# The first feed-forward product of a transformer block: left forms side by side, 512 columns to a matmul, and two of four weight sums by accumulating DMAs

## The chip, the cores and the metric

The kernel runs on one core of one Trainium2 chip. The metric is the device time of one execution in microseconds. The engines are named as the profile names them: PE (TensorE matmuls), PEld (its weight loads), DVE (VectorE), ACT (ScalarE), POOL (GpSimd) and SP (SyncE, which issues most DMAs).

## What is computed

One residual block over 512 tokens with 2048 features, in float32: two kinds of attention, then a feed-forward part, then a norm. The change concerns the feed-forward part:

```python
h2 = rmsnorm(x, g_mlp[l])
u = jax.nn.relu(jnp.einsum('bsd,df->bsf', h2, w_up[l]))     # 512 x 2048 times 2048 x 8192
x = x + jnp.einsum('bsf,fd->bsd', u * u, w_down[l])         # 512 x 8192 times 8192 x 2048
return rmsnorm(x, g_final)
```

## The kernel before

**Numbers.** Every float32 factor is split into a high half (the value rounded to the type that PE multiplies, made by a copy on ACT, L60) and a low half (the rest, made by a subtraction on DVE, L61, which waits for the copy). A product is then three matmuls that add into the same PSUM tile: high x high, low x high and high x low (`mm3`, L92 to L95). The program's scheduler sets the order in which each engine's instructions stand, and each engine runs its own in that order.

**First feed-forward product.** It uses seven products in place of eight (Strassen's scheme in Winograd's form). The left factor is the transposed activation, cut in four blocks and combined to seven forms by `a_form` (L449 on), one for each product `p`. Each form has a tile of high halves `fh{p}` and one of low halves `fl{p}`, both [128, 8, 256]: 8 chunks of the sum, 256 columns (tokens). They are made at the end of the output projection and stay for the whole product.

The right factor is `w_up`, taken in 32 units (`Unit`) of 256 columns each. A unit loads two raw tiles `wu` of 1 MB: b11 and b12 side by side in one, b21 and b22 in the other (five such buffers, pool `rw`; the first tile of unit 0 is two tiles `wq`). `Unit.product(p)` does one of the seven products: it makes the weight sum in place on DVE if the form needs one (p = 5, 6, 4, 7 at L557, L559, L561, L563), splits the sum into `wh` and `wl` (or `wx`, a fourth pair of buffers), multiplies (8 chunks x 3 matmuls of 256 columns into the accumulators `psa`, `psb` or `psc`), and combines the results. Products 1, 6, 7 and 4 add up in `psa`, which ACT copies out after 1, 6 and 7 (L572) and 4 (L582); DVE adds the copies to `psb` or `psc` (L578, L580, L584). The four results are rectified and squared on ACT (L585, L586).

The loop over units does product 1 of the new unit, 4 of the old one, 5 and 6 of the new, 3 of the old, 2 and 7 of the new. Between them `store_form` makes the forms for the second feed-forward product from each pair of units and stores them to DRAM (`ufd<-st`), so DVE, ACT and SP's DMA queue have that work as well.

**Around it.** Ahead of it stands the output projection (PSUM tiles `acco`), in four column blocks; at the end of each the residual tile `x2` is transposed, scaled to `hr`, turned into forms, and squared on ACT into a tile `junk` for the norm's sums (L509). Behind it comes the second feed-forward product (`accd`), with 512 columns to a matmul.

Of the kernel before, what the change touches and what calls it, by code (L numbers as in the profile page):

```python
# [35 lines left out]
def block_kernel(ctx, tc, x, g_attn, w_in, b_f, g_out_sb, g_out_fox, w_out, g_mlp, w_up, w_down, g_final, y):  # L36
# [407 lines left out]
    F = {p: tuple(form.tile([P, KC // 2, 2 * P], F32R, tag=f"f{c}{p}", name=f"f{c}{p}") for c in "hl") for p in range(1, 8)}  # L444
# [7 lines left out]
    def a_form(p, c, out, s=None):  # L452
# [4 lines left out]
        if p == 5:  # L457
            dve.tensor_tensor(s, a21, a22, op=ALU.add)
# [4 lines left out]
        if p == 3:  # L463
            dve.tensor_tensor(a12, a12, s, op=ALU.subtract)
# [4 lines left out]
    for n in range(4):  # L469
# [33 lines left out]
        for p in (1, 5, 6, 2, 7, 4, 3):  # L503
            if n == 3 and p == 4:
                break
            a_form(p, hr, [f[:, 2 * n:2 * n + 2, :] for f in F[p]], s12)
        for t in range(TB):
            junk = xp.tile([P, NT], F32, tag="junk", name="junk")
            act.activation(junk, x2[:, t, :], AF.Square, accum_out=ss2[:, t, n:n + 1])  # L509
# [7 lines left out]
    rw = ctx.enter_context(tc.tile_pool(name="rw", bufs=5, side="right", reuse_waits="tile"))  # L517
    ups_cm = tc.tile_pool(name="ups", bufs=2, space=PSUM, reuse_waits="tile")
# [11 lines left out]

    class Unit:
        def __init__(self, u):
            self.u = u
            cols = slice(2 * u * P, 2 * (u + 1) * P)
            rows_ = w_up.rearrange("(a i p) f -> i p a f", i=2, p=P)
            if u == 0:
# [10 lines left out]
            self.A, self.B, self.C = (ups.tile([P, NT], F32, tag=c, name=f"ps{c}")[:, :2 * P] for c in "abc")  # L547

        def product(self, p):
# [6 lines left out]
            if p == 5:  # L556
                dve.tensor_tensor(b11, b12, b11, op=ALU.subtract)  # L557
            if p == 6:
                dve.tensor_tensor(b11, b22, b11, op=ALU.subtract)  # L559
            if p == 4:  # L560
                dve.tensor_tensor(b21, b21, b11, op=ALU.subtract)  # L561
            if p == 7:
                dve.tensor_tensor(b12, b22, b12, op=ALU.subtract)  # L563
# [3 lines left out]
            for a in range(KC // 2):  # L567
                mm3(ps, hi[:, a, :], lo[:, a, :], F[p][0][:, a, :], F[p][1][:, a, :], a == 0 and p in (1, 2, 5), a == KC // 2 - 1)
            t1, t2 = slice(0, 2 * P), slice(2 * P, NT)
            if p in (1, 6, 7):  # L570
                self.m = sm.tile([P, 2 * P], F32, tag="m6" if p == 6 else "m", name=f"s{p}", bufs=2 if p == 6 else 1)
# [3 lines left out]
                if p == 1:  # L575
                    self.m1 = self.m
            if p == 7:
                dve.tensor_tensor(self.c[:, 1, t2], self.m, self.C, op=ALU.add)  # L578
# [289 lines left out]
```

## Time and profile before

| | |
|---|---|
| runs of the kernel | 2093.0, 2093.42, 2095.84 us; median 2093.42 |
| profiled execution | span 2090.6 us from the first to the last instruction; the median run is 2.8 us above it |
| output projection with its forms | about 640 to 829 us |
| first feed-forward product | about 829 to 1465 us |
| second feed-forward product | about 1465 to 2024 us |
| granted PE clock | 1.00 in these stages |

A group's row in the profile gives the line, the engine, the operation, out<-in with sizes, the count, the busy time, the mean duration of one, and then the engine's idle time just before with what ended it. Matmuls are pipelined, so the duration of one is longer than the interval from one to the next. In the kernel's sums a stream's interval is therefore taken: a stretch divided by the matmuls in it.

### The profile page before, as it was taken

To read this page: it belongs to the slowest core of one execution; us is meant where nothing else is said; L and a number is where in the kernel's file an instruction comes from. 1 tells how busy PE (TensorE), PEld (TensorE's weight loads), DVE (VectorE), ACT (ScalarE), POOL (GpSimd) and SP (SyncE) were. 2 spreads that over 40 slices of the span, in tenths; PEclk is the share of its full clock that TensorE was granted. 3 is DMA by queue.
4 is the path that set the end of the run, shared out by engine and by line. 5 is a ranking of instruction groups with operands and counts; after the bars stand their busy time and mean duration, and the time that the engine had idled before them with its cause. 6 is when DMAs were issued, how large, how long until landed. Compare 5 with 4: busy or idle time off the path is not lost.

```text
span 2090.6 us, 29838 instructions
## 1 busy us (share of the span) xinstructions
PE 2070.1 (99%) x12084; PEld 1841.0 (88%) x12084; DVE 1570.7 (75%) x1744; ACT 1034.2 (49%) x1396; POOL 52.9 (3%) x76
## 2 busy tenths in 40 slices
PE   9999999999999999999999999999999999999998
PEld 8888888888898888999999999999888888888886
DVE  5454545665677567888888888888798988888886
ACT  6333334444445555556665666666744443333433
POOL 0000000010000000000000000000000000000003
PEclk9999999999999999999999999999999999999999
DMA  6323332323323444466566566567856664663732
GB/s 193 81 87 85 83 89 72 90 75 87 81 81 111 147 145 152 138 206 192 185 219 189 185 205 205 176 201 248 299 201 251 249 225 172 249 250 134 271 111 81
DMA packets 239930, 339.68 MB, mean 162 GB/s; under 512 B 7936, under 2 KB 154416, under 8 KB 233776
## 3 DMA queue, kind: packets, MB, share of 16 engines
q1 hardware_dynamic: 238832, 335.64, 48.9%
q8 instruction: 95, 1.56, 0.3%
q10 hardware_dynamic: 960, 2.13, 0.3%
q14 instruction: 43, 0.35, 0.0%
HBM read 272.20 MB, written 65.54 MB: 162 GB/s over the span
## 4 chain that ended last, share of the span: by engine, by line
PE 98%; DVE 1%; ACT 0%; issue 0%; DMA 0%; SPq 0%; ACTq 0%
PE accd L93 8%; PE accd L94 8%; PE accd L95 8%; PE psa L94 6%; PE psa L93 6%; PE psa L95 6%; PE accq L95 6%; PE accq L94 6%; PE accq L93 6%; PE psc L94 3%; PE psc L95 3%; PE psc L93 3%; PE acco L95 3%; PE acco L94 3%; PE acco L93 3%; PE accv L93 3%
## 5 line engine op out<-in xcount | busy, mean ns | idle before, releaser
L60 ACT CAST wh<-wu 128x1024 fp32r<-128x1024 f32 x164 | 170.9, 1048 | 134.8 <-PE psa L94 55.3
L61 DVE TENSOR_TENSOR wl<-wu,wh 128x1024 fp32r<-128x1024 f32 x164 | 199.4, 1221 | 45.0 <-ACT wh L60 44.7
L94 PE MATMUL psa<-fl,wh 128*128 128x256 f32 x776 | 219.8, 283 | 1.8 <-DVE fl L61 1.8
L93 PE MATMUL psa<-fh,wh 128*128 128x256 f32 x776 | 219.9, 283 | 0.5 <-ACT s L572 0.5
L95 PE MATMUL psa<-fh,wl 128*128 128x256 f32 x776 | 219.7, 283 | 0.0
L61 DVE TENSOR_TENSOR wl<-wraw,wh 128x1024 fp32r<-128x1024 f32 (+2 forms) x133 | 158.7, 1194 | 80.1 <-ACT wh L60 73.8
L60 ACT CAST wh<-wd 128x1024 fp32r<-128x1024 f32 (+1 forms) x136 | 134.6, 999 | 168.6 <-PE accd L95 107.5
L60 ACT CAST wh<-wraw 128x1024 fp32r<-128x1024 f32 (+2 forms) x133 | 135.4, 1019 | 156.5 <-PE accq L94 77.6
L95 PE MATMUL accq<-hH,wl 128*128 128x512 f32 x512 | 200.4, 391 | 0.0
L93 PE MATMUL accq<-hH,wh 128*128 128x512 f32 x512 | 200.1, 391 | 0.0
L94 PE MATMUL accq<-hL,wh 128*128 128x512 f32 x512 | 200.0, 391 | 0.0
L61 DVE TENSOR_TENSOR wl<-wd,wh 128x1024 fp32r<-128x1024 f32 (+1 forms) x136 | 155.5, 1153 | 41.9 <-ACT wh L60 41.4
L93 PE MATMUL accd<-wh,uf 128*128 128x512 f32 x436 | 169.7, 389 | 0.9 <-issue 0.9
L94 PE MATMUL accd<-wl,uf 128*128 128x512 f32 x436 | 169.6, 389 | 0.0
L95 PE MATMUL accd<-wh,uf 128*128 128x512 f32 x436 | 169.6, 389 | 0.0
L94 PEld LDWEIGHTS psa<-fl,wh 128*128 128x128 f32 x776 | 149.0, 192 | 2.2 <-DVE fl L61 2.2
L60 ACT CAST wx<-wd 128x1024 fp32r<-128x1024 f32 (+1 forms) x88 | 87.5, 1000 | 127.3 <-PE accd L95 75.9
L93 PEld LDWEIGHTS psa<-fh,wh 128*128 128x128 f32 x776 | 149.0, 192 | 1.0 <-ACT s L572 0.7
L95 PEld LDWEIGHTS psa<-fh,wl 128*128 128x128 f32 x776 | 149.0, 192 | 0.2 <-DVE wl L61 0.2
L61 DVE TENSOR_TENSOR wx<-wd,wx 128x1024 fp32r<-128x1024 f32 (+1 forms) x88 | 100.7, 1153 | 23.6 <-ACT wx L60 23.2
L94 PEld LDWEIGHTS accq<-hL,wh 128*128 128x128 f32 x512 | 96.2, 188 | 19.5
L95 PEld LDWEIGHTS accq<-hH,wl 128*128 128x128 f32 x512 | 96.1, 188 | 19.3
(300 smaller groups left out, 5491.9 us busy)
## 6 DMA issues: line engine op xcount, KB each, us to landing
wu<-in_w_up_dram SPq DMA_DIRECT2D x63, 1024.0 KB, 6.7
ufd<-st SPq DMA_DIRECT2D x98, 512.0 KB, 6.8
wd<-in_w_down_dram SPq DMA_DIRECT2D x48, 1024.0 KB, 6.1
wraw<-in_w_in_dram SPq DMA_DIRECT2D x84, 512.0 KB, 3.7
uf<-ufd SPq DMA_DIRECT2D x42, 1024.0 KB, 5.9
wraw<-in_w_out_dram SPq DMA_DIRECT2D x32, 512.0 KB, 3.6
wd<-in_w_down_dram SPq DMA_DIRECT2D x16, 768.0 KB, 6.2
uf<-ufd SPq DMA_DIRECT2D x14, 768.0 KB, 5.6
```

What stands on the lines that cost most here:

```text
L60: ins = act.copy(hi, src)
L61: lows[0] = dve.tensor_tensor(lo, src, hi.bitcast(F32), op=ALU.subtract)
L93: pe.matmul(out, sh, mh, start=first, stop=False, skip_group_check=True)
L94: pe.matmul(out, sh, ml, start=False, stop=False, skip_group_check=True)
L95: pe.matmul(out, sl, mh, start=False, stop=last, skip_group_check=True)
```

## The change

```diff
-    F = {p: tuple(form.tile([P, KC // 2, 2 * P], F32R, tag=f"f{c}{p}", name=f"f{c}{p}") for c in "hl") for p in range(1, 8)}
+    F = {p: tuple(form.tile([P, KC // 4, 2, 2 * P], F32R, tag=f"f{c}{p}", name=f"f{c}{p}") for c in "hl") for p in range(1, 8)}
+
+    def form_parts(p, n):
+        pair = F[p][n // 2][:, 2 * (n % 2):2 * (n % 2) + 2]
+        return pair[:, :, 0, :], pair[:, :, 1, :]
...
-    def a_form(p, c, out, s=None):
+    def a_form(p, c, out, s=None, sums=False):
...
-            dve.tensor_tensor(s, a21, a22, op=ALU.add)
+            dve.tensor_tensor(s, a21, a22, op=ALU.subtract if sums else ALU.add)
...
-            dve.tensor_tensor(a12, a12, s, op=ALU.subtract)
+            dve.tensor_tensor(a12, a12, s, op=ALU.add if sums else ALU.subtract)
...
-            a_form(p, hr, [f[:, 2 * n:2 * n + 2, :] for f in F[p]], s12)
+            a_form(p, hr, form_parts(p, n), s12, True)
         for t in range(TB):
-            junk = xp.tile([P, NT], F32, tag="junk", name="junk")
-            act.activation(junk, x2[:, t, :], AF.Square, accum_out=ss2[:, t, n:n + 1])
+            act.activation(x2[:, t, :], x2[:, t, :], AF.Square, accum_out=ss2[:, t, n:n + 1])
...
+    def add_dma(out, src):
+        for h in (slice(0, KC // 4), slice(KC // 4, KC // 2)):
+            pool.dma_start(out[:, h, :], src[:, h, :], accum_op=ALU.add)
...
+            self.w12 = rows_[0][:, :, (2 * u + 1) * P:2 * (u + 1) * P]
...
-            self.A, self.B, self.C = (ups.tile([P, NT], F32, tag=c, name=f"ps{c}")[:, :2 * P] for c in "abc")
+            self.A, self.B, self.C = (ups.tile([P, NT], F32, tag=c, name=f"ps{c}") for c in "abc")
...
             if p == 5:
-                dve.tensor_tensor(b11, b12, b11, op=ALU.subtract)
+                add_dma(b11, self.w12)
             if p == 6:
-                dve.tensor_tensor(b11, b22, b11, op=ALU.subtract)
+                dve.tensor_tensor(b11, b22, b11, op=ALU.add)
             if p == 4:
-                dve.tensor_tensor(b21, b21, b11, op=ALU.subtract)
+                dve.tensor_tensor(b21, b21, b11, op=ALU.add)
             if p == 7:
-                dve.tensor_tensor(b12, b22, b12, op=ALU.subtract)
+                add_dma(b12, b22)
...
             for a in range(KC // 2):
-                mm3(ps, hi[:, a, :], lo[:, a, :], F[p][0][:, a, :], F[p][1][:, a, :], a == 0 and p in (1, 2, 5), a == KC // 2 - 1)
+                both = F[p][a // 4][:, a % 4].rearrange("p s c -> p (s c)")
+                pe.matmul(ps, hi[:, a, :], both, start=a == 0 and p in (1, 2, 5), stop=False, skip_group_check=True)
+                pe.matmul(ps[:, :2 * P], lo[:, a, :], both[:, :2 * P], start=False, stop=a == KC // 2 - 1, skip_group_check=True)
...
-                self.m = sm.tile([P, 2 * P], F32, tag="m6" if p == 6 else "m", name=f"s{p}", bufs=2 if p == 6 else 1)
+                self.m = (sr if p == 6 else sm).tile([P, NT], F32, tag="m", name=f"s{p}", bufs=2 if p == 6 else 1)
...
+            def sums(out, m):
+                dve.tensor_tensor(out, m[:, t1], m[:, t2], op=ALU.add)
+
             if p == 7:
-                dve.tensor_tensor(self.c[:, 1, t2], self.m, self.C, op=ALU.add)
+                dve.tensor_tensor(self.m, self.C, self.m, op=ALU.subtract)
+                sums(self.c[:, 1, t2], self.m)
             if p == 2:
-                dve.tensor_tensor(self.c[:, 0, t1], self.m1, self.B, op=ALU.add)
+                dve.tensor_tensor(self.m1, self.m1, self.B, op=ALU.add)
+                sums(self.c[:, 0, t1], self.m1)
             if p == 4:
-                act.copy(self.c[:, 0, t2], self.A)
+                act.copy(self.c[:, 0, t2], self.A[:, t1])
+                dve.tensor_tensor(self.c[:, 0, t2], self.c[:, 0, t2], self.A[:, t2], op=ALU.add)
             if p == 3:
-                dve.tensor_tensor(self.c[:, 1, t1], self.m6, self.C, op=ALU.add)
+                dve.tensor_tensor(self.m6, self.C, self.m6, op=ALU.subtract)
+                sums(self.c[:, 1, t1], self.m6)
```

What it does, part by part. The high and low halves of a left form now lie side by side in one tile, [high 256 | low 256] for each chunk, so one matmul of 512 columns multiplies the weights' high half by both; a second one of 256 columns multiplies the weights' low half by the form's high half. An accumulator is 512 wide: its two halves must still be added, which DVE does at each of the four results. The sums for products 5 and 7 become DMAs issued on POOL that add into the tile in SBUF, each in two parts of four chunks (256 KB): for product 5 the other operand is read again from `w_up` in DRAM, for product 7 it is the tile b22. Such a DMA can add but not subtract, so the signs of the forms, of the other two sums and of the combinations are turned accordingly. The squares for the norm are written over the residual tile.

The scheduler puts the instructions into a new order. On DVE in unit 6, from product 1's low half (the first row) to product 5's low half (the last), the kernel before has these rows (`wu` raw weights, `s` the copies of `psa`, `c` the results):

```order
L61 TENSOR_TENSOR wl_7975<-wu_7967,wh_7974 128x1024 [waits PE_49,Activation_49]
L584 TENSOR_TENSOR c_7661<-s6_7628,psc_7500 128x256 [waits PE_49]
L61 TENSOR_TENSOR wx_8011<-wu_7730,wx_8011 128x1024 [waits Activation_49]
L557 TENSOR_TENSOR wu_7967<-wu_7967 128x8x128 [waits DVE_49]
L580 TENSOR_TENSOR c_7661<-s1_7762,psb_7733 128x256 [waits PE_49]
L563 TENSOR_TENSOR wu_7967<-wu_7969,wu_7967 128x8x128 [waits DMAHW6_49,DVE_49]
L61 TENSOR_TENSOR st_8068<-c_7194,st_8068 128x512 [waits DMAHW7_49,DMAHW0_49,Activation_49]
L61 TENSOR_TENSOR wl_8041<-wu_7967,wh_8040 128x1024 [waits Activation_49]
```

and the changed kernel these, with the sum for product 6 behind them:

```order
L61 TENSOR_TENSOR wl_7676<-wu_7668,wh_7675 128x1024 [waits DMAHW5_49,PE_49,Activation_49]
L598 TENSOR_TENSOR s1_7505<-s1_7505,psb_7484 128x512 [waits PE_49]
L61 TENSOR_TENSOR wx_7704<-wu_7481,wx_7704 128x1024 [waits Activation_49]
L592 TENSOR_TENSOR c_7425<-s1_7505 128x256 [waits DVE_49]
L595 TENSOR_TENSOR s7_7664<-psc_7485,s7_7664 128x512 [waits Activation_49]
L592 TENSOR_TENSOR c_7425<-s7_7664 128x256 [waits DVE_49]
L61 TENSOR_TENSOR wl_7728<-wu_7668,wh_7727 128x1024 [waits DMASW3_49,DMASW2_49,Activation_49]
L570 TENSOR_TENSOR wu_7668<-wu_7670,wu_7668 128x8x128 [waits DVE_49]
```

The two sums at L557 and L563 are gone from DVE. Product 5's low half now waits for the two DMAs (DMASW) in place of an operation of DVE's own, and five other operations stand between it and product 1's.

On POOL the kernel before has nothing in this stage. The changed one has the adding DMAs of all units in one queue; here are those of units 5 (`wu_7479`) and 6 (`wu_7668`), where the source `wu` marks a sum for product 7 and `in_w_up_dram` one for product 5:

```order
L539 DMA wu_7479<-wu_7481 128x4x128 [waits DMAHW7_49,DMAHW3_49,DMASW4_49]
L539 DMA wu_7479<-wu_7481 128x4x128 [waits DMASW5_49]
L539 DMA wu_7668<-wu_7670 128x4x128 [waits DMAHW5_49,DMAHW6_49,DMASW6_49,DVE_49]
L539 DMA wu_7668<-wu_7670 128x4x128 [waits DMASW7_49]
L539 DMA wu_7479<-in_w_up_dram 128x4x128 [waits DMASW0_49,DVE_49]
L539 DMA wu_7479<-in_w_up_dram 128x4x128 [waits DMASW1_49]
L539 DMA wu_7668<-in_w_up_dram 128x4x128 [waits DMASW2_49,DVE_49]
L539 DMA wu_7668<-in_w_up_dram 128x4x128 [waits DMASW3_49]
```

Unit 6's sum for product 7 stands ahead of unit 5's sum for product 5, and waits for unit 6's loads (DMAHW). So it is in one unit of four; in the others each unit's two sums stand together, product 7's first.

More of the change, by code (lines that the diff above doesn't have):

```diff
@@ L517, in block_kernel @@
     rw = ctx.enter_context(tc.tile_pool(name="rw", bufs=5, side="right", reuse_waits="tile"))
+    sr_cm = tc.tile_pool(name="sr", bufs=2, side="right", reuse_waits="tile")
+    sr = sr_cm.__enter__()
     ups_cm = tc.tile_pool(name="ups", bufs=2, space=PSUM, reuse_waits="tile")
@@ L699, in block_kernel @@
                 for q in (4, 3):
-                    a_form(q, hr, [f[:, 6:, :] for f in F[q]], s12)
+                    a_form(q, hr, form_parts(q, 3), s12, True)
                 xp_cm.__exit__(None, None, None)
@@ L711, in block_kernel @@
     ups_cm.__exit__(None, None, None)
+    sr_cm.__exit__(None, None, None)
     mps2_cm = tc.tile_pool(name="mps2", bufs=1, space=PSUM, side="right", reuse_waits="tile")
```

## The prediction

> **What bounds the kernel now.** I read the profile page first, then busy time by stage, then single rows of the stage that the change touches.
>
> ```profile
> span 2090.6 us, 29838 instructions
> ...
> PE 2070.1 (99%) x12084; PEld 1841.0 (88%) x12084; DVE 1570.7 (75%) x1744; ACT 1034.2 (49%) x1396; POOL 52.9 (3%) x76
> ...
> PE 98%; DVE 1%; ACT 0%; issue 0%; DMA 0%; SPq 0%; ACTq 0%
> ```
>
> TensorE is busy nearly always and is 98% of the chain that ended last. So a gain must come out of PE's own time, and any wait that reaches PE is a loss. The rows by stage (for each engine busy us and instructions, then granted clock, DMA share, GB/s) are, in this order, the first feed-forward product, the second one, a stage of projections, and the output projection:
>
> ```profile
> 870.00:1441.00 571.00, 571.00 (x4760) 571.00 (x4760) 488.99 (x555) 349.83 (x469) 0.00 (x0) 1.00 0.61 193
> 1600.00:1800.00 200.00, 200.00 (x884) 165.58 (x884) 174.86 (x133) 82.28 (x83) 0.00 (x0) 1.00 0.62 227
> 240.00:300.00 60.00, 60.00 (x279) 50.20 (x278) 37.06 (x60) 22.97 (x40) 1.63 (x4) 1.00 0.28 80
> 640.00:829.00 189.00, 185.94 (x895) 156.14 (x894) 126.85 (x171) 105.21 (x174) 0.00 (x0) 1.00 0.44 150
> ```
>
> The first row has no idle PE, at clock 1.00. Its matmuls are 256 columns wide: 571 / 4760 = 120.0 ns each. The second row has only 512-column ones: 200 / 884 = 226.2 ns. So 256 more columns cost 106.2 ns and every matmul carries 13.8 ns beside its columns. The durations of 283 and 391 ns in the groups overlap; only these intervals may be summed.
>
> ```profile
> L93 PE MATMUL psa<-fh,wh 128*128 128x256 f32 x776 | 219.9, 283 | 0.5 <-ACT s L572 0.5
> ...
> L93 PE MATMUL psa<-fh,wx 128*128 128x256 f32 x248 | 70.2, 283 | 0.0
> ```
>
> 776 + 248 = 1024 triples go into accumulator A: 32 units x 4 products x 8 chunks. With B and C there are 32 x 7 x 8 = 1792 triples. One unit is 56 of them: 168 x 0.120 = 20.16 us. In it DVE works 488.99 / 571 x 20.16 = 17.26 us and ACT 61% of the time.
>
> **The change on PE.** A triple (3 x 120.0 = 360.0 ns) becomes one 512- and one 256-column matmul: 226.2 + 120.0 = 346.2 ns. The columns stay 768; one fixed part of 13.8 ns goes. 1792 x 13.8 ns = **-24.7 us**, and a unit becomes 19.39 us. No row alternates the two widths. If changing over cost another fixed part, the gain would be 0; if both remaining parts vanished too, it would be 74 us. I take 24.7, because both uniform streams show the same fixed part.
>
> **The change on DVE and ACT.** These starts give what one operation takes from DVE in a stream:
>
> ```profile
> 1029.06 1.22 DVE L557 TENSOR_TENSOR wu<-wu 128x1024 f32<-128x1024 f32 x1
> 1030.20 0.41 DVE L584 TENSOR_TENSOR c<-s,psc 128x256 f32<-128x256 f32 x1
> 1030.54 1.22 DVE L61 TENSOR_TENSOR wl<-wu,wh 128x1024 fp32r<-128x1024 f32 x1
> 1031.67 1.22 DVE L563 TENSOR_TENSOR wu<-wu 128x1024 f32<-128x1024 f32 x1
> ...
> 1038.58 0.68 DVE L458 TENSOR_TENSOR c<-c 128x512 f32<-128x512 f32 x1
> 1039.18 1.22 DVE L61 TENSOR_TENSOR wl<-wu,wh 128x1024 fp32r<-128x1024 f32 x1
> ```
>
> 1024 elements take 1.14 us (1029.06 to 1030.20), 256 take 0.34, 512 take 0.60. A unit loses two weight sums, 2 x 1.14 = 2.28. It gains three combinations that are 512 wide in place of 256 (3 x 0.26 = 0.78), three adds of the two halves (3 x 0.34) and one add for product 4 (0.34): 2.14. DVE's total is therefore unchanged: 17.26 - 0.14 = 17.1 us, now in a unit of 19.39. ACT's three copies double in width, some 0.25 us each, and its 39% idle time covers them. Flipping the signs of the forms and laying the two halves side by side adds no instruction; I cost both at 0, covered by the same engines as before. If that cover went, DVE would still have 2.3 us a unit.
>
> **The new wait.** The sum for product 5 is now two accumulating DMAs issued on POOL. They may start only when product 1's low half has been read on DVE (that split reads the same tile), and product 5's cast on ACT and its low half on DVE wait for them. Both engines work in order, so everything behind that cast waits too: the splits of products 6, 2 and 3, which PE needs next. The rows of unit 6 in the order section show what DVE does meanwhile: 0.60 + 1.14 + 0.34 + 0.60 + 0.34 = 3.0 us. Counted alike, the later units have 1.9 to 7.2 us there, 4.7 on average. Call L the time from the low half of product 1 to the landing of both adds. DVE then runs in a ring: its 17.1 us, less the 4.7 that lie beside the add, plus L, plus the cast.
>
> ```profile
> 1018.23 2.00 ACT L60 CAST wh<-wu 128x1024 fp32r<-128x1024 f32 x2
> ```
>
> Two casts take 2.00, one 1.0 us. The ring is 17.1 - 4.7 + 1.0 + L = 13.4 + L. PE sets the pace as long as this is at most 19.39, that is while **L is at most 6.0 us**; at L = 6.8 the ring takes the old 20.16 us and the gain is gone; each us more costs 32.
>
> The trace has no POOL DMA and no accumulating DMA. The nearest rows (KB each, median us from issue to landing):
>
> ```profile
> wu<-in_w_up_dram SPq DMA_DIRECT2D x63, 1024.0 KB, 6.7
> ufd<-st SPq DMA_DIRECT2D x98, 512.0 KB, 6.8
> ...
> wraw<-in_w_in_dram SPq DMA_DIRECT2D x84, 512.0 KB, 3.7
> ...
> ufd<-st SPq DMA_DIRECT2D x14, 256.0 KB, 6.4
> ...
> wq<-in_w_up_dram SPq DMA_DIRECT2D x2, 512.0 KB, 4.0
> ```
>
> The add moves 512 KB in two parts. Its bounds are 3.7 us (512 KB in a quiet stage) and 12.8 (two 256 KB stores of this stage, one after the other). I take 5.4, halfway between 4.0 (the same 512 KB of the same tensor) and 6.8 (512 KB in this stage, but queued behind loads on SP's queue, which the add is not). The ring is then 18.8 us and PE stays the bound.
>
> The Trainium skill (DMA: Bandwidth & Descriptors, Anatomy of one DMA — SWDGE (gpsimd) path) fits 2.0 us plus bytes / 436e3 to a DMA issued there: 2.6 us for each half, 3.2 to 5.2 for both, an estimate from that page. By it nothing would be lost and the sum would be -24.7. No row here shows such a DMA.
>
> The sum for product 7 needs only the loaded tiles and comes a good unit earlier; its own wait costs 0. But in one unit of four it stands in POOL's queue ahead of the preceding unit's product-5 add (the second order fence), and it waits for a load that DVE's last read of an older tile releases. Between that read and the end of product 1's low half the order has 4.2 us of DVE work. With 6.7 us for the load, 2 us for the two adds ahead (an estimate: 1024 packets at the 29 ns worked out below, on 16 engines), L = 5.4 and the cast, DVE waits 6.7 + 2 + 5.4 + 1.0 - 4.2 - 7.2 = 3.7 us in that unit, of which the ring's spare time in the other three (3 x 0.6) covers 1.8. Eight such units cost between 0 and 8 x 1.9 = 15 us. I take **+6**.
>
> **The seam and the rest.** Before the first unit PE idles 189 - 185.94 = 3.1 us in the fourth stage row. Two DVE sums leave that place (-2.3 at most); the four squares now write over the residual tile, so they wait for the transposes and the store, and stand on ACT among the last forms (+3 at most, four of the next row's 0.63 with their accumulator reads).
>
> ```profile
> 813.08 0.63 ACT L509 ACTIVATE junk<-x 128x512 f32<-128x512 f32 x1 [0.64 <-DVE x L487]
> ```
>
> I count 0, with both ends kept. The second product and the attention don't change: 0.
>
> **Sum.** -24.7 + 6 + 0 = -18.7 us, on the profiled span of 2090.6: 2071.9. The median of the runs, 2093.42, lies 2.8 us above the span; with the same 2.8 around it the forecast is **2075 us**.
>
> **The rivals.**
> *The add becomes the ring (slower).* Place: DVE and ACT, in order, between products 1 and 5. It decides from L = 6.8. For it: the stores of this stage land after 6.8 us, an add reads two sources, and loads already fill 0.61 of the DMA engines. Against it: the same bytes land in 4.0 at the seam. At L = 7.5 the ring is 20.9 us, 32 x (20.9 - 20.16) = +24 us, and the reversed queue adds its 6 to 15: about 2123; at L = 8, about 2140.
>
> *The DMA engines become the bound.* A unit now keeps all 16 busy for 0.61 x 20.16 = 12.3 us. The two adds bring 2048 packets of 512 B. The projections (mostly such packets) pay 0.28 x 16 / 80e3 us per byte, 29 ns a packet: 2048 x 29 / 16 = 3.7 us, 16.0 of 19.39, no bound. If the second read doubles that, 12.3 + 7.4 = 19.7 us: a unit at best 0.5 below today's, -15 us, and transfers that queue for each other, which lengthens L too: about 2090 (2079 to 2105). The Trainium skill (Collectives: The Full Stack, The bandwidth ceiling: the fold count and why AG ≠ RS ≠ AR) says just that: an add in the DMA path costs no cycles itself but needs two source reads on one ring, so it runs at half the rate of a copy. No run here shows it yet; by it this rival holds, by the plain packet price the forecast.
>
> *POOL's issuing.* Four issues a unit; above 19.39 / 4 = 4.85 us each, POOL sets the pace: at 6 us, 32 x (24 - 20.16) = +123, 2216. Nothing in the trace speaks for or against it.
>
> *The change of width eats the gain.* The PE term is 0 and the waits stay: 2093 to 2099.
>
> **How the numbers follow.** Forecast 0.48, own range 2064 to 2084 (by the seam, the reversed queue and an add between 3.7 and 6.2 us). Add as the ring 0.34. DMA engines 0.10. POOL 0.04. Width 0.04. Two kernels of this length can be told apart by about 0.2%, 4.2 us: faster is below 2089.2, slower above 2097.6. Faster: 0.48 + 0.04 of the DMA rival = 0.52. Same: 0.03 of that, 0.02 of the ring near its threshold, 0.02 of the width = 0.07. Slower: 0.41. The range runs from 2064 to 2140: it leaves out 0.04 below, the POOL rival and the longest adds (0.12).
>
> **What would show it.** Right: the unit stage has intervals that average 173 ns a matmul, no idle PE, and lasts 25 us less; ACT's wait for the adds at product 5 is a few us and PE's waits on `wh` stay near zero. Wrong: DVE or ACT wait for the add in every unit and PE has a gap before each product 5; the add lands later than 6.8 us after its issue; the DMA share in the stage is above 0.9; POOL is busy more than 4.8 us for an issue; or PE, though never waiting, takes 360 ns a pair.

## The result and the profile after

| | |
|---|---|
| before | 2093.67 us, median of 4 runs |
| after | 2446.97 us, median of 4 runs (2442.06 to 2450.68) |
| ratio | 1.1686, 95% interval 1.1669 to 1.1702 |
| profiled execution after | span 2443.9 us (before: 2090.6) |

The change costs 353 us where the prediction had -18. The page of the changed kernel answers to the lines quoted from the page of before (span, engines, chain of waits, the adding queue, and POOL's two kinds of DMA with KB and median us from issue to landing):

```profile
span 2443.9 us, 26666 instructions
...
PE 2141.0 (88%) x10292; PEld 1792.2 (73%) x10292; DVE 1570.6 (64%) x1808; ACT 1049.6 (43%) x1396; POOL 219.2 (9%) x204
...
q0 software_dynamic: 67584, 33.56, 11.1%
...
PE 64%; issue 12%; DMA 9%; DVE 9%; ACT 4%; POOL 2%; ACTq 0%; DVEq 0%; POOLq 0%; SPq 0%
...
wu<-wu POOLq DMA_DIRECT2D x62, 256.0 KB, 3.9
wu<-in_w_up_dram POOLq DMA_DIRECT2D x62, 256.0 KB, 5.1
```

PE was 98% of the chain and is 64%. DVE's total is the same 1571 us: as much work, spread over a longer time. By stage (the busy times of each engine, then granted clock, DMA share, GB/s; first and second feed-forward product):

```profile
870.00:1441.00 571.00, 412.96 (x2084) 344.93 (x2083) 318.31 (x397) 239.72 (x308) 97.41 (x75) 0.84 0.68 160
2000.00:2200.00 200.00, 200.00 (x884) 165.59 (x883) 176.58 (x132) 79.51 (x78) 0.00 (x0) 1.00 0.61 212
```

The loss lies in the first feed-forward product: PE is busy 413 of 571 us there, and no other engine is near its limit; the DMA engines are at 0.68. From its first matmul to the first one of the second product, the stage grew from 654.5 to 995.4 us (+341). The other 12 us of the 353 lie around it: 7.5 before its first matmul, 3.3 in the second product, 1.6 at the end. What is waited for in the window of the first row (total us, times, longest us):

```profile
DVE wl L61 <- ACT wh L60: 176.1, 29, 16.6
...
ACT wh L60 <- DMA wu<-in_w_up_dram: 144.4, 14, 16.2
PEld psc L580 <- ACT wh L60: 130.7, 19, 15.8
PE psc L580 <- ACT wh L60: 123.6, 18, 15.5
```

Read from below: PE waits for product 5's cast on ACT, that waits for the adds from `w_up`, and DVE waits behind it. One unit in the timelines of POOL, ACT and DVE (start, duration, and in brackets the idle time ahead with what ended it):

```profile
1114.64 1.29 POOL L539 DMA_DIRECT2D wu<-in_w_up_dram  x1 [16.83 <-DVE wl L61]
1122.44 1.30 POOL L539 DMA_DIRECT2D wu<-in_w_up_dram  x1 [6.50 <-issue]
1127.53 1.29 POOL L539 DMA_DIRECT2D wu<-wu  x1 [3.79 <-issue]
1131.71 1.30 POOL L539 DMA_DIRECT2D wu<-wu  x1 [2.89 <-issue]
```

```profile
1127.30 1.04 ACT L60 CAST wh<-wu 128x1024 fp32r<-128x1024 f32 x1 [6.63 <-DMA wu<-in_w_up_dram]
```

```profile
1113.01 1.23 DVE L61 TENSOR_TENSOR wl<-wu,wh 128x1024 fp32r<-128x1024 f32 x1
...
1118.88 0.42 DVE L592 TENSOR_TENSOR c<-s 128x256 f32<-128x256 f32 x1
1128.37 1.22 DVE L61 TENSOR_TENSOR wl<-wu,wh 128x1024 fp32r<-128x1024 f32 x1 [9.07 <-ACT wh L60]
1129.63 1.22 DVE L570 TENSOR_TENSOR wu<-wu 128x1024 f32<-128x1024 f32 x1
```

Product 1's low half ends at 1114.24, and the first half of the add is issued 0.4 us later, which takes POOL 1.29 us. **The second half is issued only at 1122.44**, though it waits for nothing of the first and POOL is idle for 6.50 us ("issue": nothing that the profile shows). By the records of landing, the first half landed 0.31 us before that, and so it is everywhere: of the 64 second halves of this run every one starts 0.26 to 0.32 us after the first has landed. The second lands at about 1127.2, the cast starts, and DVE has waited 9.07 us. So L, from the end of product 1's low half to the last landing, is 13.0 us in this unit. Over all 32 units these records give **L = 15.5 us** on average: 13.4 for the pair, and 2.1 in which the pair stands in POOL's queue (6 to 8 in the units with the reversed order, where L is 18 to 23.5; 0.4 in nearly all others).

### The profile page after: what moved, and what is told of

It is laid out like the page before. It is cut to its first block, busy times and chain, and to the rows that moved or that the text cites. A ratio compares the mean times of both kernels' runs of the same rounds, so it can differ in the third digit from the quotient of the medians.

```text
span 2443.9 us, 26666 instructions
## 1 busy us (share of the span) xinstructions
PE 2141.0 (88%) x10292; PEld 1792.2 (73%) x10292; DVE 1570.6 (64%) x1808; ACT 1049.6 (43%) x1396; POOL 219.2 (9%) x204
## 3 DMA queue, kind: packets, MB, share of 16 engines
q0 software_dynamic: 67584, 33.56, 11.1%
## 4 chain that ended last, share of the span: by engine, by line
PE 64%; issue 12%; DMA 9%; DVE 9%; ACT 4%; POOL 2%; ACTq 0%; DVEq 0%; POOLq 0%; SPq 0%
DMA wu<-in_w_up_dram 7%; PE accd L94 6%; PE accd L95 6%; PE accd L93 6%; PE accq L95 5%; PE accq L94 5%; PE accq L93 5%; PE psc L580 3%; DVE wl L61 3%; PE psa L580 3%; ACT wh L60 2%; PE acco L94 2%; PE acco L93 2%; PE acco L95 2%; PE accv L93 2%
## 5 line engine op out<-in xcount | busy, mean ns | idle before, releaser
L580 PE MATMUL psc<-fh,wh 128*128 128x512 f32 x188 | 99.2, 540 | 213.4 <-ACT wh L60 213.1
L580 PEld LDWEIGHTS psc<-fh,wh 128*128 128x128 f32 x188 | 47.8, 254 | 232.2 <-ACT wh L60 224.3
L580 PE MATMUL psa<-fh,wh 128*128 128x512 f32 x388 | 149.3, 416 | 6.9 <-ACT s L585 6.7
L580 PE MATMUL psa<-fl,wh 128*128 128x512 f32 x388 | 143.8, 404 | 0.0
L539 POOL DMA_DIRECT2D wu<-in_w_up_dram x62 | 80.6, 1300 | 516.6 <-DVE wl L61 263.4
L61 DVE TENSOR_TENSOR wx<-wu,wx 128x1024 fp32r<-128x1024 f32 x56 | 68.4, 1221 | 80.3 <-ACT wx L60 80.1
L581 PE MATMUL psa<-fh,wl 128*128 128x256 f32 x388 | 112.2, 289 | 0.0
L94 PE MATMUL accd<-wx,uf 128*128 128x512 f32 x284 | 110.6, 389 | 0.1
```

Source lines behind the costliest of these rows:

```text
L61: lows[0] = dve.tensor_tensor(lo, src, hi.bitcast(F32), op=ALU.subtract)
L94: pe.matmul(out, sh, ml, start=False, stop=False, skip_group_check=True)
L539: pool.dma_start(out[:, h, :], src[:, h, :], accum_op=ALU.add)
L580: pe.matmul(ps, hi[:, a, :], both, start=a == 0 and p in (1, 2, 5), stop=False, skip_group_check=True)
L581: pe.matmul(ps[:, :2 * P], lo[:, a, :], both[:, :2 * P], start=False, stop=a == KC // 2 - 1, skip_group_check=True)
```

## The experiments

Times are medians, beside 2093.3 us of the kernel before in the same sessions. Theory A, from the start on: the two halves can't be in flight together, since the memory that the kernel reserves for POOL's DMA descriptors holds only one of them.

### How the adds are issued: e1, e15, e3, e2

```diff
-    nc = _bacc.Bacc("TRN2", target_bir_lowering=False, num_devices=1, dynamic_dma_scratch_size=2048)
+    nc = _bacc.Bacc("TRN2", target_bir_lowering=False, num_devices=1, dynamic_dma_scratch_size=3072)
```

> Edit: the memory reserved for POOL's DMA descriptors (dynamic_dma_scratch_size) 3072 in place of 2048, nothing else. Theory A (the reserved memory holds one of these adds but not two, so POOL can't issue the next until the one before has landed): the second half now starts about 1.3 us after the first (the time of one issue), no longer 0.31 us after the first has landed; a pair for product 5 lands in about 7 to 8 us in place of 12.6; POOL's serial queue of about 23 us a unit falls to about 12, the unit from 30.4 to 20 to 23 us, the time from 2447 to between 2090 and 2210. Theory B (adding DMAs follow one another whatever memory is reserved, for instance since each adds on one queue): the 0.31 us after landing stays in all pairs, and the time stays within 1% of 2447.

Measured: 2275.07 us, ratio 1.086 (1.0835 to 1.0886). POOL's timeline in this run and, below it, in e15 (2560 reserved):

```profile
1043.10 1.29 POOL L539 DMA_DIRECT2D wu<-in_w_up_dram  x1 [1.57 <-DVE st L61]
1044.59 1.31 POOL L539 DMA_DIRECT2D wu<-in_w_up_dram  x1 [0.20 <-issue]
1065.95 2.60 POOL L539 DMA_DIRECT2D wu<-in_w_up_dram  x2 [20.06 <-DVE wl L61]
```

```profile
1042.28 1.30 POOL L539 DMA_DIRECT2D wu<-in_w_up_dram  x1 [1.57 <-DVE st L61]
1043.77 1.31 POOL L539 DMA_DIRECT2D wu<-in_w_up_dram  x1 [0.19 <-issue]
```

> Edit: the changed kernel with 2560 reserved for POOL's descriptors. Theory A (room for two adds or for one): 2560 has room for two where 2048 just has not (e3 had three quarters in flight in 2048, so a half takes between 683 and 2048 of it, and e1 at least two halves in 3072, so at most 1536): if a half takes 1280 or less, the second half starts 1.3 us after the first as in e1, and the time is e1's, 2255 to 2290; if more, the starts stay 0.31 us after the landings, 2447. A time in between, with halves that overlap in part, would speak for a cause that scales with the memory and not for a count of adds.

Measured: 2282.16 us, one run. In both, the halves are issued one right behind the other, and never after a landing. A quarter more of memory does what a half more does: it is a count of adds, not the memory as such. But only half of the loss is gone: a pair for product 5 still takes 9.5 us (9.7 in e15), not the 7 to 8 of the expectation, for two halves that are under way together each take longer: 7.5 us at the median, against 5.1 one at a time.

e3 splits each sum into four DMAs of 128 KB:

```diff
-        for h in (slice(0, KC // 4), slice(KC // 4, KC // 2)):
+        for h in (slice(i, i + 2) for i in range(0, KC // 2, 2)):
```

> Edit: each sum as four DMAs of 128 KB in place of two of 256 KB. Theory A: a DMA of half the size needs half the descriptors, so the reserved memory holds two or three of them: the second starts 1.3 us after the first, the third when the first has landed, a set for product 5 lands in 8 to 10 us in place of 12.6, and the time falls to 2200 to 2350. Theory B: all four follow one another, each with its fixed part, at 3 to 4 us each: a set takes 12 to 16 us and the time is 2447 or longer, up to 2560.

Measured: 2351.83 us, one run, just above theory A's range; a set took 11.7 us. POOL's timeline at the first sum has three issues at once and the fourth apart:

```profile
804.42 3.84 POOL L539 DMA_DIRECT2D wq<-in_w_up_dram  x3 [173.21 <-DVE wl L61]
809.86 1.22 POOL L539 DMA_DIRECT2D wq<-in_w_up_dram  x1 [1.60 <-issue]
```

The fourth starts 0.26 us after the first of them has landed. So 2048 holds three quarters but one half, and 2560 two halves: if the needs of several adds simply add up, one half takes more than 1024 and at most 1280 of it.

e2 lets the same DMAs copy:

```diff
-            pool.dma_start(out[:, h, :], src[:, h, :], accum_op=ALU.add)
+            pool.dma_start(out[:, h, :], src[:, h, :])
```

> Edit: the POOL DMAs copy in place of adding, at the same place with the same bytes and waits (the sums for products 5 and 7 are left out of the computation). Theory A: a copy needs half the descriptors of an add, so two are in flight: the second half starts about 1.3 us after the first; packets cost about 29 ns in place of 64; a pair lands in 5 to 7 us; time 2075 to 2150. Theory B in its form for adds alone: the same, so this run doesn't tell them apart. Theory B in its form for all POOL DMAs: the second half starts 0.31 us after the first has landed here too; a pair takes 7 to 10 us, time 2150 to 2350.

Measured: 2169.75 us, one run, slower than theory A's range. The halves overlap in 2048 (second start 0.74 us after the first at the median). The queue's row against the changed kernel's 67584 packets and 11.1%:

```profile
q0 software_dynamic: 10240, 33.56, 4.2%
...
wu<-wu POOLq DMA_DIRECT2D x62, 256.0 KB, 2.6
wu<-in_w_up_dram POOLq DMA_DIRECT2D x62, 256.0 KB, 5.6
```

The same 33.56 MB take 0.042 x 16 x 2168.0 = 1457 us of DMA engine time as a copy and 0.111 x 16 x 2443.9 = 4340 as an add, three times as much: the add goes in packets of some 500 B at 64 ns each, the copy in packets of 3.3 KB at 142 ns. Yet even a copy's pair takes 6.8 us here.

### The ring: e7, e8, e16, e17

e7 and e8 give product 7's sum back to DVE; e8 also reserves 3072.

```diff
-                add_dma(b12, b22)
+                dve.tensor_tensor(b12, b22, b12, op=ALU.add)
```

> Edit: product 7's sum on DVE, product 5's by DMA, so POOL's queue holds nothing ahead of product 5's adds and no unit's order is reversed. Ring theory: 13.4 + 1.1 (the sum back on DVE) + L with the serial pair's 12.6 us = 27.1 us a unit, 32 x (27.1 - 20.16) = +222: about 2315 (2270 to 2340); the difference to 2447 is the price of product 7's adds in the queue, reversed ones above all. Rival (product 5's wait alone explains the changed kernel): 2400 or more.

Measured: 2406.93 us, one run: the rival. Product 7's adds in the queue cost only 40 us of the 353.

> Edit: as the last, with 3072 reserved for POOL's descriptors, so the two halves overlap. Ring theory: L falls to 7 to 9 us (pairs took 9.5 on average with product 7's adds about), the ring to 21.5 to 23.5 us a unit: 2135 to 2200. If the overlap doesn't shorten L (the engines move no more at once): as without it, about 2315.

Measured: 2244.94 us, one run. Longer than the 2200 expected. Its stage is 156.5 us shorter than e7's, for an L that is 4.9 us shorter: 32 units x 4.9. That led to this table, all from the records of the traces and rounded at the end: L, the part of L in which DVE works, and the stage from its first matmul to the first one of the second product.

| run | L | DVE busy in L | stage | stage / 32 | stage / 32 - L |
|---|---|---|---|---|---|
| e2, copies | 7.3 | 4.9 | 726.0 | 22.7 | 15.4 |
| e8 | 9.5 | 5.9 | 800.5 | 25.0 | 15.6 |
| e1 | 10.4 | 5.2 | 829.5 | 25.9 | 15.6 |
| e15 | 10.6 | 5.2 | 836.4 | 26.1 | 15.6 |
| e7 | 14.3 | 6.0 | 957.0 | 29.9 | 15.6 |
| changed kernel | 15.5 | 5.1 | 995.4 | 31.1 | 15.6 |
| e16 | 17.9 | 7.4 | 999.4 | 31.2 | 13.4 |
| e17 | 12.1 | 7.6 | 816.4 | 25.5 | 13.4 |

In the first six rows **a unit takes 15.6 us + L** (15.4 with the copies), over a range of L of two to one: the ring of the prediction, with a constant of 15.6 in place of 13.4. The last two rows move product 5 behind two others and ask for both sums' adds right behind product 1, e17 with 3072 and the matmuls grouped as in e9 below:

```diff
-            if p == 5:
-                add_dma(b11, self.w12)
...
-            if p == 7:
-                add_dma(b12, b22)
...
+            if p == 1:
+                add_dma(b11, self.w12)
+                add_dma(b12, b22)
...
-        for i, (who, p) in enumerate(((new, 1), (old, 4), (new, 5), (new, 6), (old, 3), (new, 2), (new, 7))):
+        for i, (who, p) in enumerate(((new, 1), (old, 4), (old, 3), (new, 2), (new, 5), (new, 6), (new, 7)) if u else [(new, p) for p in (1, 5, 6, 2, 7)]):
```

> Edit: the changed kernel with product 5 moved behind the old unit's product 3 and the new one's product 2 (order 1, old 4, old 3, 2, 5, 6, 7), both sums' DMAs asked for right behind product 1. Matmuls not grouped, 2048 reserved as in the changed kernel. Ring theory: three products' splits and combinations, some 7.5 us of DVE's 17.1, now lie beside the add in place of next to nothing, so the unit is about 8 + L; with L of 14 to 16 (serial halves) 22 to 24 us: 2150 to 2230, against 2447. Rival (the adds cost by what they do to the DMA engines or to POOL's queue, not by the place of the wait): above 2350.

Measured: 2447.52 us, one run, the changed kernel's time to the microsecond. It looks like the rival, but the table says otherwise: the scheduler put only 2.3 us more of DVE's work beside the add (7.4 for 5.1), not 7.5, and the constant fell by about that, to 13.4. L grew by 2.4 us, nearly all of it since product 7's adds, now asked for with product 5's, stand ahead of them more often (4.4 us of queue in place of 2.1), and this took the gain back. So the run moved too little to test the place of the wait by its time alone.

> Edit: e16 with grouped matmuls and 3072 reserved. Ring theory: 8 + L with L of about 10 is 18 us, under PE's 19.5, so PE sets the pace as in e9: 2080 to 2095, and it beats both kernels if the adds cost nothing else. If they do (as in e13, where sums meant to be early still were waited for, because the loads ahead of them come late): 2100 to 2150.

Measured: 2260.47 us, ratio 1.0799 (1.0785 to 1.0814). The expectation fell for the same reason: 13.4 + 12.1 = 25.5 us a unit, far above PE's.

### The rest of the change without the adds: e4, e5, e9, e12

> Edit: all four weight sums on DVE again, with the changed signs; the wide matmuls, the halves side by side and the squares in place stay. My theory of the time lost (the serial adds, and no other part of the change): PE waits for nothing as before, its granted clock is back at 1.00, a triple takes 346 ns; DVE works 17.1 + 2.3 = 19.4 us a unit, as long as PE's 19.39, so some of the gain is lost to DVE: 2070 to 2090. Rival (the wide matmuls or the extra combinations cost time by themselves, and the clock of 0.84 is theirs): 2100 or more, or a clock below 0.95 in the stage.

Measured: 2121.45 us, ratio 1.0137 (1.012 to 1.0153). A miss: with no add by DMA at all the change still loses 28 us. e5 leaves out these two sums:

```diff
-                add_dma(b11, self.w12)
+                pass
...
-                add_dma(b12, b22)
+                pass
```

> Edit: the sums for products 5 and 7 are left out of the computation altogether, no DMA and no DVE operation in their place; all else as in the changed kernel. This is the prediction's kernel with an add that takes no time (L = 0). If PE's and DVE's terms of the prediction hold: PE never waits, DVE works 17.1 us a unit, and the stage lasts 18 to 25 us less than before (a triple is 350 ns by the starts in the run with all sums on DVE, not 346.2): 2068 to 2080. Rival (what cost the run with all sums on DVE its 28 us is not DVE's 19.4 us a unit but the longer chain behind each product, with copies of 512 columns and two more adds, which holds psa): PE still waits for the copies of psa, and the time is 2095 to 2120.

Measured: 2092.01 us, ratio 0.9992 (0.9982 to 1.0001). **With L = 0 the change gains nothing either.** e9 keeps that and puts the matmuls of one width together:

```diff
                 pe.matmul(ps, hi[:, a, :], both, start=a == 0 and p in (1, 2, 5), stop=False, skip_group_check=True)
+            for a in range(KC // 2):
+                both = F[p][a // 4][:, a % 4].rearrange("p s c -> p (s c)")
                 pe.matmul(ps[:, :2 * P], lo[:, a, :], both[:, :2 * P], start=False, stop=a == KC // 2 - 1, skip_group_check=True)
```

> Edit: as e5 (the sums for products 5 and 7 left out of the computation), and in every product the eight matmuls of 512 columns come first, then the eight of 256. e5's unit took 19.8 us, 353 ns for a pair of matmuls (starts: 236 and 117), where the prediction had 346.2. If the change of width at every matmul costs the 7 ns: a pair takes 346 ns again, the unit 19.4 us, the time falls by up to 12 us below e5's 2092: 2078 to 2086. If a 512-column matmul is slower in this stage whatever stands beside it: 236 or so in the run of eight, the time stays within 4 us of 2092.

Measured: 2079.31 us, ratio 0.9933 (0.9918 to 0.9948). The unit stage of e5 and of e9, first by window (PE's busy time and matmuls come first):

```profile
870.00:1441.00 571.00, 567.36 (x3209) 491.05 (x3208) 490.85 (x617) 365.72 (x474) 0.00 (x0) 1.00 0.62 198
```

```profile
870.00:1441.00 571.00, 569.94 (x3264) 501.20 (x3263) 498.57 (x629) 369.41 (x483) 0.00 (x0) 1.00 0.63 203
```

A pair takes 2 x 567.36 / 3209 = 353.6 ns where the width changes at every matmul and 2 x 569.94 / 3264 = 349.2 where it changes after eight; the prediction had 346.2. So the frequent change costs 4.4 ns a pair, 1792 x 4.4 = 7.9 us, and 3.0 ns more are in neither stream of before (the changes that e9 keeps are among them). The granted clock is 1.00 in both, so the 0.84 of the changed kernel belongs to its idle PE and not to the wide matmuls. DVE works 490.85 / 571 x 19.8 = 17.0 us a unit, as predicted. In e5 the stage is 6.6 us shorter than before, and 5.0 of it are lost in the second product, whose start waits on ACT (waits between 1455 and 1500 us of e5; none of these stands in the same place before):

```profile
ACT xr L688 <- DMA xr<-xd: 6.2, 2, 3.8
...
PEld accd L93 <- ACT m L678: 3.3, 1, 3.3
PE accd L93 <- ACT m L678: 2.8, 1, 2.8
```

The scheduler now puts the scaling of a residual tile ahead of ACT's copies of the first results, 12.5 us after the second product's start (before: 18.4), and its load comes too late for that.

e12 is e4 with grouped matmuls.

> Edit: as e4 (all sums on DVE), with the eight 512-column matmuls of a product ahead of its eight 256-column ones, so PE needs a product's low half, DVE's last step, some 1.9 us later. If PE's waits of e4 are for DVE's and ACT's work at the start of a product, it drops from 2121 to 2095 to 2110; if DVE's total of 19.4 us a unit is the bound, it stays within 5 us of 2121.

Measured: 2097.56 us, ratio 1.002 (1.001 to 1.0029): 24 us below e4, twice what grouping gave without the sums (12.7). So the two sums on DVE cost 29 us with alternating widths (e4 against e5) and 18 grouped (e12 against e9). What PE waits for in e4's stage:

```profile
PE psa L580 <- ACT s L585: 15.3, 8, 2.5
...
PE psc L581 <- DVE wl L61: 1.2, 1, 1.2
```

So most of it is for ACT's copies of the accumulator `psa`, as the rival of e5's expectation had it, and little for a low half that PE needs right behind the high one. In e12 the wait for the copies is 5.4 us, and none for a low half shows. By which path grouping shortens it wasn't followed, and the 18 us that stay weren't divided between DVE's total and the order of its work.

### The sums in other places: e10, e11, e6, e13, e14, e18

e10 lets POOL add both sums itself, e11 product 7's alone (product 5's on DVE):

```diff
-                add_dma(b11, self.w12)
+                pool.tensor_tensor(b11, b12, b11, op=ALU.add)
...
-                add_dma(b12, b22)
+                pool.tensor_tensor(b12, b22, b12, op=ALU.add)
```

> Edit: the two sums as additions that POOL computes itself, in place of its DMAs. Its 128x512 addition elsewhere took 1.30 us, so 128x1024 takes about 2.6 and L is about 3, under the 6.0 us at which the ring sets the pace. If L is all that the changed kernel loses beyond e5: the time is e5's, 2090 to 2100. Rival (POOL's additions slow DVE's, which read and write the same memory at the same time): 2105 to 2150, and DVE's 128x1024 operations, 1.22 us now, take longer beside POOL's.

Measured: 2155.14 us, ratio 1.0285 (1.0268 to 1.0302): the rival, 5 us above its range. Groups of POOL and of DVE in e10 (busy us, mean ns of one), then two of DVE's in e4:

```profile
L568 POOL TENSOR_TENSOR wu<-wu 128x1024 f32<-128x1024 f32 x31 | 81.0, 2612 | 516.2 <-DVE wl L61 365.6 <-DVE wx L61 150.6
```

```profile
L61 DVE TENSOR_TENSOR wl<-wu,wh 128x1024 fp32r<-128x1024 f32 x136 | 193.0, 1430 | 12.6 <-ACT wh L60 12.5
...
L469 DVE TENSOR_TENSOR c<-c 128x512 f32<-128x512 f32 x13 | 21.7, 1672 | 0.0
...
L604 DVE TENSOR_TENSOR s<-psc,s 128x512 f32<-128x512 f32 x25 | 17.2, 688 | 17.7 <-PE psc L581 17.7
```

```profile
L604 DVE TENSOR_TENSOR s<-psc,s 128x512 f32<-128x512 f32 x27 | 18.6, 688 | 2.3 <-PE psc L581 2.3
...
L469 DVE TENSOR_TENSOR c<-c 128x512 f32<-128x512 f32 x14 | 9.7, 692 | 0.0
```

POOL's own 2.6 us are as expected. But DVE's 128x512 operation on two SBUF tiles (L469) goes from 692 to 1672 ns, and the split from 1223 to 1430 on average. These means mix two cases, which the times of the records part: beside a POOL addition L469 takes 2515 ns (7 of 13) and otherwise 688, the split 2689 (18 of 135) and otherwise 1220. The operation of the same size with one operand in PSUM (L604) takes 688 on average, and no longer in the 13 of 25 that lie beside an addition. All 50 operations on two SBUF tiles that began during an addition ended 0.3 to 1.1 us behind its end; the 6 that began ahead of one took their usual 1220 ns. DVE is then busy 536 of the 571 us (521 in e4), and PE waits 26.9 us for low halves. The Trainium skill (GPSIMD Engine Reference, 1. Specifications) says that POOL shares its SBUF interfaces with VectorE and contends with instructions that have two SBUF inputs; this trace agrees, to the kind of operation.

> Edit: product 5's sum on DVE, product 7's as an addition that POOL computes. DVE works 18.3 us a unit and nothing waits for a DMA. If the load on DVE is what the run with all sums on DVE (2121) lost by: 2093 to 2105, near e5. If the length of the chain between products is: about 2115. e6 (product 7's by DMA) took 2164; if its 2164 comes from the adding DMAs, this one is well below it.

Measured: 2159.02 us, ratio 1.0315 (1.0299 to 1.033), a miss. Two causes show: DVE's splits take 1335 ns on average (3470 in the 6 of 133 beside a POOL addition), and POOL's addition can start only when DVE's sum for product 5 has read b12 (it waited 422.7 us for that). How much each costs wasn't separated. e6 has the same dependence, with adding DMAs:

> Edit: product 5's sum on DVE, product 7's by DMA as in the changed kernel. The adds for product 7 come a unit early; two serial ones take about 8.5 us and nobody waits for them. If DVE's load is what the run with all sums on DVE lost by: DVE 18.3 us a unit in place of 19.4, 2085 to 2105. If the adds disturb the rest (their packets slow the loads and stores): above 2121.

Measured: 2164.34 us, ratio 1.0338 (1.0322 to 1.0353), a miss. Its waits in the stage:

```profile
ACT wh L60 <- DMA wu<-wu: 64.6, 10, 9.7
PEld psa L580 <- ACT wh L60: 36.9, 6, 7.3
PE psa L580 <- ACT wh L60: 35.0, 6, 7.0
```

The adds no longer come a unit early, as they do in the changed kernel, where product 5's other operand comes from DRAM; a serial pair takes 11.8 us, and product 7 waits for it. e13 takes that dependence away, with the matmuls grouped: product 6's sum is made from product 7's, product 5's from product 6's, behind product 2:

```diff
+            if p == 1:
+                add_dma(b12, b22)
+            if p == 6:
+                dve.tensor_tensor(b11, b12, b11, op=ALU.add)
             if p == 5:
-                add_dma(b11, self.w12)
-            if p == 6:
-                dve.tensor_tensor(b11, b22, b11, op=ALU.add)
-            if p == 4:
                 dve.tensor_tensor(b21, b21, b11, op=ALU.add)
-            if p == 7:
-                add_dma(b12, b22)
+                dve.tensor_tensor(b11, b11, b22, op=ALU.subtract)
...
-        for i, (who, p) in enumerate(((new, 1), (old, 4), (new, 5), (new, 6), (old, 3), (new, 2), (new, 7))):
+        for i, (who, p) in enumerate(((new, 1), (old, 4), (new, 6), (old, 3), (new, 2), (new, 5), (new, 7))):
```

> Edit: matmuls grouped as in e12; product 7's sum by DMA at the start of the unit, with nobody else reading b12 before it; product 6's sum made from it (b11 + b12), product 5's from product 6's (b11 - b22), and product 5 moved behind product 2. No instruction waits for a fresh add: it has some 15 us before its first reader. DVE works 18.3 us a unit. If only a short L is what keeps the changed kernel from its gain: PE sets the pace at 19.5 us a unit as in e9, and the time is 2079 to 2090, below the kernel before. If the adding DMAs cost time even where no sum waits in a ring (their packets delay the unit's loads and the stores): 2100 to 2140.

Measured: 2176.69 us, ratio 1.0405 (1.039 to 1.0419), a miss. Its waits:

```profile
POOL wu L539 <- DMA wu<-in_w_up_dram: 153.6, 12, 23.8
...
DVE wu L570 <- DMA wu<-wu: 62.4, 11, 8.2
```

My premise was wrong: the adds aren't early, since POOL waits for the unit's loads, which come only shortly before they are used, and a serial pair then takes 13.7 us. So this run doesn't tell what adds cost that nobody waits for.

> Edit: as e13 with 3072 reserved for POOL's descriptors. If the adds in e13 are early enough: the same within 3 us. If they are late there by being serial: faster than e13 by more than 5 us.

Measured: 2145.57 us, ratio 1.0246 (1.0232 to 1.026). 31 us faster: they are late there, in part by being serial.

> Edit: e6 (product 5's sum on DVE, product 7's by DMA) with grouped matmuls and 3072 reserved. In e6 product 7's adds could start only when DVE's sum for product 5 had read b12, and a pair took 11.8 us. With halves that overlap a pair takes about 6.4: ACT's 83 us of waiting for them nearly goes, and the grouped order gives 12 to 24 us as in e9 and e12: 2085 to 2105. If other waits of the queue stay: 2110 to 2140.

Measured: 2094.38 us, ratio 1.0003 (0.9994 to 1.0012): the time of before, and the best version with all sums and an adding DMA. From 830 us to the stage's end ACT waits 24.0 us for the adds, at most 2.9 at a time, where e6's ACT waits 82.7 and up to 9.7, and PE's one wait for such a cast there is 2.1 us. Two edits are in it at once; how the 70 us divide between them wasn't measured.

No version with all sums in it beats the kernel before.

## Why the prediction was wrong

**L was taken as 5.4 us and is 15.5.** This is the step that failed, and the largest. "Halfway between 4.0 and 6.8" treats the two halves as one transfer of 512 KB. They are two, and the second is issued after the first has landed: with the shortest adds of the trace, 3.8 us each, that alone gives 7.9. The upper bound of 12.8 was worked out from just that ("one after the other"), for another reason, and was given too little weight; even it is below 15.5, for the queue behind other adds comes on top. e1 and e15 show the serial issue by taking it away: in e1 L falls by 5.1 us and the stage by 166, 5.2 a unit. Of the 10.4 us that are left in e1, 0.9 are queue and 9.5 the pair itself: an add in this stage is slow, where two plain copies in the same place take 6.8. Why, beyond the larger time of its packets, wasn't separated.

**The ring itself was right, its constant 2.2 us too low.** DVE's 17.1 us a unit measured 17.0, the 4.7 beside the add 5.1. But 13.4 allowed DVE no idle time except one cast. In the changed kernel it also waits for other results, here in the window of 571 us:

```profile
DVE s L595 <- ACT s L585: 17.7, 13, 2.1
...
DVE s L604 <- PE psc L581: 6.4, 8, 3.3
...
DVE s L598 <- PE psb L581: 6.0, 10, 2.8
```

With 3.0 us of smaller ones that is 33 us in 18.4 units, 1.8 us a unit: 17.0 - 5.1 + 1.0 + 1.8 = 14.7, and 0.9 of the 15.6 stay unaccounted for. Counted like the table, a unit of before takes 654.5 / 32 = 20.5 us, so the add was allowed 20.5 - 15.6 = 4.9 us before the old pace is lost, not 6.8. If the line of the table holds below its shortest L (7.3), even my own 5.4 would have given a loss, 32 x 0.5 = 16 us. Nor do the plain copies' 7.3 fit: the place was too tight for every kind of DMA measured here.

**PE's term was -24.7 us and is -11.5.** The pair takes 353.6 ns and not 346.2: 1792 x (360.0 - 353.6) = 11.5. That "both uniform streams show the same fixed part" was no support: two intervals always fit one fixed part and one price of a column. The rival "the change of width eats the gain" held for about a third of it (7.9 us, e9), the rest is 3.0 ns a pair that neither width shows by itself.

**The seams were counted as 0.** Before the first unit the kernel without sums (e5) starts its matmuls 1.3 us later, and the second product takes 5.0 longer. Its stage is 6.6 us shorter and not 11.5, since PE idles 8.3 us in it (3.7 before). That leaves nothing of the gain at L = 0.

**The reversed queue** was given +6 us; giving product 7's sum back to DVE saved 40 (e7), with some more work on DVE. The mechanism was right, its size too small: the pair waits 6.1 to 8.2 us in POOL's queue in the units with that order and 0.4 in nearly all others.

**The rivals.** "The add becomes the ring" is what happened; its prices stopped at L = 8, since I took L from rows of other queues. "The DMA engines become the bound" did not: their share is 0.68, and 0.81 in e1; that transfers queue for each other and lengthen L fits the 7.5 us of two adds at a time, but no run shows it alone. The Trainium skill's rule on it (Collectives: The Full Stack, The bandwidth ceiling: the fold count and why AG ≠ RS ≠ AR), stated there for the adds of a reduce-scatter, that an add moves at half the rate of a copy, agrees as far as packets go (64 ns against 29 for the projections' packets), but against a real copy in the same place the add cost three times as much. The fit of 2.0 us plus bytes / 436e3 in the Trainium skill (DMA: Bandwidth & Descriptors, Anatomy of one DMA — SWDGE (gpsimd) path) gives 2.6 us for a half: the shortest copies took 2.5, the shortest adds 3.8. POOL's issuing takes 1.30 us each: that rival is out.

**The lower clock** (0.84) comes of the waits: where PE hardly waits (e5, e9), the same matmuls run at 1.00. But it isn't free. In the unit above, behind PE's wait for product 5's cast, it is 0.50 (second row; columns as in the stage rows):

```profile
1115.00:1122.00 7.00, 7.00 (x43) 6.14 (x42) 2.79 (x5) 1.18 (x2) 0.93 (x1) 1.00 0.93 230
1127.00:1133.00 6.00, 4.14 (x11) 3.17 (x12) 4.59 (x5) 4.25 (x5) 2.58 (x2) 0.50 0.35 44
```

By the records of the stage 381 matmuls run at 0.50 and take 330 ns each, the others 177: 58 us of PE's time. Little of that reaches the ring: with the copies (e2) it is 12 us, and the constant there is 15.4 and not 15.6, which is 6 us in 32 units.

## What to carry to other kernels

A transfer put in the place of an in-order engine's own operation has to be priced as a latency against the slack of the loop it lands in, and that slack is what is left of a loop's time when the engine's waits for other engines are counted too, not its busy time alone. Before two DMAs are counted as overlapping, look for a row that shows two of that queue in flight; here the memory reserved for POOL's descriptors decided it. When matmuls of two widths replace three of one, put those of a width together, which here gave 12.7 us without the sums and 24 with all of them on DVE.

## What the runs showed of the hardware

- POOL's DMAs are issued one after the landing of the other when the reserved memory holds only one: 0.26 to 0.32 us after it, in all 64 pairs; with 2560 or 3072 in place of 2048 none is. Three quarters of 128 KB fit where one half of 256 KB does.
- An adding DMA of 33.56 MB took 67584 packets and 4340 us of DMA engine time, the copy of the same bytes 10240 packets and 1457 us.
- Matmuls of 512 and 256 columns in turn take 353.6 ns a pair, eight of each in turn 349.2; streams of one width (226.2 and 120.0) add up to 346.2.
- A DVE operation on two SBUF tiles that began during a POOL addition of 2.6 us ended only 0.3 to 1.1 us behind it (all 50 in e10's window, 19 of 20 in e11's; 128x512: 2515 ns in place of 688 in e10). One with a PSUM operand took no longer beside an addition (688).
- Behind PE's waits the granted clock was 0.50 (1127 to 1133 us of the changed kernel), and matmuls of that stage took 330 ns there in place of 177 on average.
